# Where the next layer's modulation is computed, and how one layer's dense products are dealt among its recurrence and attention

## The chip, the cores and the metric

The kernel runs on one core of a Trainium2 chip. The metric is device time in microseconds (us) of one execution; the times below are of whole runs, the rows of one profiled execution.

## The reference

Two trunk layers over 256 latent tokens and 256 context tokens of width 1024. A layer normalises its input with an adaptive scale and shift, projects it once (`w_in`), runs three token mixers on the result (a bidirectional RWKV recurrence, a neighbourhood attention, a differential attention), merges them through sigmoid gates, projects (`w_out`), normalises and adds to its input:

```
mod_x = silu(c) @ w_mod[l] + b_mod[l]
sh_x, sc_x, gt_x = split(mod_x, 3)
hx = rmsnorm(x, g_pre[l]) * (1 + sc_x) + sh_x
z = hx @ w_in[l]
o = three branches of z, each times silu of its own gate
y = (sum_n sigmoid(mg_n) * (o_n @ w_branch[l, n])) @ w_out[l]
x = x + gt_x * rmsnorm(y, g_post[l])
...
```

The same is done for the context tokens with `c_ctx`; the last layer leaves their output out. The scale and shift of a layer depend on `c`, `c_ctx` and weights alone, not on the layer before.

## The kernel before

All matmuls run in a float32 form that splits each weight tile in two: ScalarE (ACT) writes the high part `wh`, VectorE (DVE) the remainder `wl`, and each product takes three matmuls (`mm3`: two on `wh`, one on `wl`). Weights come as 128x512 tiles (256 KB) on SyncE's (SP's) DMA queue into six buffers `wr`. A scheduler decides the order of each engine's instructions from the order in which the program writes them; each engine then runs its queue in that order and waits where an input isn't there.

A layer is written as follows (`run`). `weave` runs a main generator, `rwkv` and then `attn`, beside a fill generator: the projections of the later branches and gates (`zs`), the next layer's gate row (`mods`) and the first two merges. Main yields a weight at each of its phases, which is a debt; the fill then emits products until their own weights (a 256-column matmul group has a fixed one) pay it. The weights stand in the table `yl`, line 142 for layer 0 and line 143 for layer 1. In it `qq` is the phase after the recurrence's inverses, `step` the chunk steps of the recurrence (two numbers: first and second half of the sequence), `diff` a unit of the differential attention (its first number goes for layer 1's two row tiles; the second is not reached there), `nd` the norm of a pair of heads (first pair, second pair). What is not dealt when main ends is emitted then.

The last merge (`merge` with b=2, the branch of the differential attention) is emitted alone: four chunks of 24 matmuls of 512 columns; each channel tile's product is gated on DVE (`th`, line 192), added on POOL into `acc`, and split into high and low parts by ACT and DVE (`merged`). `outproj` then makes the output product in four chunks of 256 columns, in each of which four `in_wo` tiles are loaded, split and multiplied; after each split it calls `ahead(i)`, i = 0 to 15. Here the next layer's modulation comes in (layer 0 only): `mod_load` loads `in_wm` tiles (128x512, 32 in all) into slots of the slab on SP's queue, and `mod_rows` is a generator of four groups of 8 steps and a tail: a step is one weight tile against the 32 columns `cs` into the PSUM tile `y`, the tail adds the bias row on DVE (line 185, `k<-y,k`), transposes it on PE (line 199, `z<-cst,k`) and writes the scales and shifts (DVE line 192, `mA`, and ACT). 36 `next` exhaust it. `derived`, some small DVE instructions and one exponential for the next layer's constants, is emitted between the last merge and the product. `late`, `residual` and `norm_row` then make the next layer's input and `stream_in` transposes it for layer 1's first projections.

```
def ahead(i):
    if i % 4 == 3 and i // 4 < (2 if last else 4):
        self.rows_load(xsrc, i // 4, xs)
    if not last:
        self.mod_load(l + 1, ws, 2 * i - 4)
        for _ in range(2 if i > 6 else 0):
            next(mod)
```

Of the kernel before, what the change touches and what calls it, by code (L numbers as in the profile page):

```python
# [134 lines left out]
class K:  # L135
    def __init__(self, tc, io, out):
        self.tc, self.nc, self.io, self.out = tc, tc.nc, io, out
        self.n = 0
        self.have = {}
        self.in_order = False  # L140

        self.yl = [dict(inv=(57, 42.0), qq=(6, 12.07), step=(6, 6), na=(2.5, 1.19), diff=(2.3, 2.9), q=(1.0, 1.0), nd=(2.75, 5), A=(0, 0), B=(0, 4), G=(0.75, 0), C=(5.6, 7.2)),
                   dict(inv=(23, 51), qq=(3.0, 1.5), step=(6, 6), na=(1.0, 2.3), diff=(4.69, 8.12), q=(1.0, 1.0), nd=(0, 2), A=(0, 0), B=(4.5, 0), G=(0.75, 0), C=(4.0, 6.0))]


    def count(self):
# [1235 lines left out]
    def run(self):  # L1382
        tc, nc, io = self.tc, self.nc, self.io
        with ExitStack() as es:
# [26 lines left out]
            xs = []  # L1411
# [9 lines left out]
            ws = []  # L1421
            self.start(0, P, xs, self.mod_rows(0, P, ws), ws)
            for l in range(L):
                last = l == L - 1
                nq = NX if last else T
                acc = [None] * 8
                PN = None if last else self.params(l + 1)
# [23 lines left out]
                fill = self.chain(self.both(mods(), zs()), self.merge(l, 0, acc, nq), self.merge(l, 1, acc, nq))  # L1451
                self.weave(self.rwkv(l, P, last), fill, False)
                self.weave(self.attn(l, P, last), fill)
                self.now(self.merge(l, 2, acc, nq))
                s = self.merged(acc, nq)
                xsrc = io["xt"] if l == 0 else self.xd

                ws, xs, late = [], [], []
                if not last:
                    self.derived(l + 1, PN)  # L1460
                    self.h_new()
                    mod = self.mod_rows(l + 1, PN, ws)

                def ahead(i):
                    if i % 4 == 3 and i // 4 < (2 if last else 4):
                        self.rows_load(xsrc, i // 4, xs)
                    if not last:
                        self.mod_load(l + 1, ws, 2 * i - 4)
                        for _ in range(2 if i > 6 else 0):
                            next(mod)  # L1470

                def rows(t, y, ss):
# [4 lines left out]
                def done(t, y, ss):  # L1477
                    if t < 2:
                        rows(t, y, ss)
                    else:  # L1480
                        late.append((t, y, ss))

                self.outproj(l, s, 1 if last else 2, ahead, done)
                if not last:
                    self.mod_load(l + 1, ws, 32)
# [68 lines left out]
```

## Time and profile before

| | |
|---|---|
| median of 3 runs | 1429.24 us (1428.95 to 1432.83) |
| profiled execution | 1424.81 us |
| its span | 1423.1 us |
| TensorE (PE) busy | 1320.4 us, 93% |
| VectorE (DVE) busy | 995.7 us, 70% |
| ScalarE (ACT) busy | 779.2 us, 55% |
| GpSimd (POOL) busy | 233.6 us, 16% |
| mean granted clock of PE | 0.966 of full speed |

Busy time is the union of an engine's instructions. The span is what the trace covers; the execution's own time holds a little more around it. On the time axis of the trace the last merge of layer 0 runs from about 737 to 759 us, the output product to about 823, layer 1's first projections begin at about 833; layer 1's recurrence steps run from about 1187, its attention ends at about 1346, and its last merge and output product follow.

### The profile page before, as it was taken

The page shows a single profiled execution, that of the slowest core. Times are in us where ns is not written, and L with a number is a line of the kernel's source. Part 1 is how long each engine was busy: PE and PEld are TensorE (multiplying, and loading weights), DVE is VectorE, ACT ScalarE, POOL GpSimd, SP SyncE. Part 2 cuts the span into 40 slices and gives each one's busy share as a digit, 9 for nine tenths or more (in the row PEclk, how much of TensorE's full clock was granted, in tenths as well). Part 3 has the DMA queues.
Part 4 walks back from the last instruction along what each step waited for, and adds up shares of the span by engine and source line. Part 5 has one row for each costly group of instructions (what it writes and reads, how often), then busy time and mean ns, then how long its engine had stood idle before and what let it go on. Part 6 is the DMA issues. An engine that isn't in the chain of part 4 may idle for free. (4 is left out here: it accounts for less than half of the span.)

```text
span 1423.1 us, 28637 instructions
## 1 busy us (share of the span) xinstructions
PE 1320.4 (93%) x10784; PEld 1098.9 (77%) x10784; DVE 995.7 (70%) x2117; ACT 779.2 (55%) x1734; POOL 233.6 (16%) x292
## 2 busy tenths in 40 slices
PE   6998999999999999998999889998999999999897
PEld 4866777889779876677778777888878789867687
DVE  4763469836898368778685386768848893679886
ACT  5462375336863446667433255866449634467653
POOL 0010011012110012224253000101111000122441
PEclk9999999999999999999999999999889999999899
DMA  9466642424324267432545844354513252685454
GB/s 356 129 196 200 208 130 82 128 68 157 119 80 121 77 185 222 155 105 93 178 145 168 324 127 119 113 177 126 170 56 105 68 148 69 182 272 154 141 166 154
DMA packets 112987, 212.42 MB, mean 149 GB/s; under 512 B 13088, under 2 KB 24880, under 8 KB 112848
## 3 DMA queue, kind: packets, MB, share of 16 engines
q1 hardware_dynamic: 102896, 178.33, 40.6%
q0 software_dynamic: 9952, 32.26, 7.0%
q8 instruction: 85, 1.39, 0.4%
q14 instruction: 54, 0.44, 0.1%
HBM read 176.70 MB, written 33.83 MB: 148 GB/s over the span
## 5 line engine op out<-in xcount | busy, mean ns | idle before, releaser
L195 PE MATMUL z<-k,wh 128*128 128x512 f32 (+1 forms) x2352 | 653.9, 361 | 8.8 <-ACT wh L164 4.2
L195 PEld LDWEIGHTS z<-k,wh 128*128 128x128 f32 x2352 | 417.8, 194 | 76.2 <-issue 9.1
L195 PE MATMUL z<-k,wl 128*128 128x512 f32 (+1 forms) x1176 | 421.7, 360 | 7.3 <-DVE wl L185 7.3
L164 ACT ACTIVATE wh<-wr 128x512 fp32r<-128x512 f32 x376 | 235.4, 630 | 317.8 <-PE z L195 212.7
L185 DVE TENSOR_TENSOR wl<-wr,wh 128x512 fp32r<-128x512 f32 x376 | 278.5, 747 | 157.7 <-PE z L195 59.9
L195 PEld LDWEIGHTS z<-k,wl 128*128 128x128 f32 x1176 | 227.1, 194 | 42.8 <-DVE wl L185 12.1
L195 PE MATMUL z<-wh,k 128*128 128x256 f32 x736 | 145.1, 291 | 2.6 <-ACT k L164 1.3
L195 PEld LDWEIGHTS z<-wh,k 128*128 128x128 f32 x736 | 119.6, 196 | 5.7 <-DVE k L192 2.1
L195 PE MATMUL z<-wl,k 128*128 128x256 f32 x368 | 106.7, 290 | 0.6 <-DVE wl L185 0.6
L185 POOL TENSOR_TENSOR k<-k,k 64x512 fp32r<-64x512 f32 (+3 forms) x64 | 78.0, 1222 | 154.9 <-ACT k L164 62.1
L164 ACT ACTIVATE gs<-z 128x512 f32<-128x512 f32 (+1 forms) x134 | 66.7, 500 | 53.5 <-PE z L195 44.1
L164 ACT ACTIVATE k<-k 64x256 fp32r<-64x256 f32 (+5 forms) x146 | 74.8, 537 | 32.0 <-POOL k L185 20.3
L185 DVE TENSOR_TENSOR k<-k,k 128x256 fp32r<-128x256 f32 (+5 forms) x134 | 76.0, 580 | 12.0 <-ACT k L164 9.3
L199 PE MATMUL b<-cst,k 128*128 128x128 f32 x368 | 65.1, 286 | 17.6 <-DVE k L189 5.6
L164 ACT ACTIVATE k<-a,s 128x512 f32<-128x512 f32 (+1 forms) x96 | 59.2, 617 | 33.1 <-DVE s L179 32.1
L195 PEld LDWEIGHTS z<-wl,k 128*128 128x128 f32 x368 | 72.2, 196 | 1.4 <-DVE wl L185 1.0
L199 PEld LDWEIGHTS b<-cst,k 128*128 128x128 f32 x368 | 42.9, 144 | 37.6 <-issue 15.0
L164 ACT ACTIVATE k<-b 128x256 f32<-128x256 f32 (+1 forms) x144 | 62.8, 465 | 16.5 <-PE b L199 15.8
L195 PE MATMUL a<-k,k 128*128 128x512 f32 (+1 forms) x192 | 61.1, 404 | 10.0 <-ACT k L164 6.1
L195 PE MATMUL a<-ar,bk 64*128 64x128 f32 (+1 forms) x512 | 51.1, 288 | 9.6 <-ACT Lab L164 8.8
L195 PEld LDWEIGHTS a<-ar,bk 64*128 64x128 f32 x512 | 43.5, 190 | 21.3 <-ACT Lab L164 15.7
L179 DVE TENSOR_REDUCE s<-a 128x1 f32<-128x512 f32 (+1 forms) x96 | 56.4, 588 | 1.2 <-PE a L195 1.0
(175 smaller groups left out, 1899.4 us busy)
## 6 DMA issues: line engine op xcount, KB each, us to landing
wr<-in_wi SPq DMA_DIRECT2D x296, 256.0 KB, 3.1
k<-in_wm SPq DMA_DIRECT2D x64, 256.0 KB, 5.4
wr<-in_wb SPq DMA_DIRECT2D x48, 256.0 KB, 2.6
md<-gs SPq DMA_DIRECT2D x36, 256.0 KB, 2.9
k<-md POOLq DMA_DIRECT2D x36, 256.0 KB, 4.5
wr<-in_wg SPq DMA_DIRECT2D x32, 256.0 KB, 3.4
wr<-in_wo SPq DMA_DIRECT2D x32, 256.0 KB, 4.0
gd<-gs SPq DMA_DIRECT2D x18, 256.0 KB, 3.2
```

The lines of the kernel that those rows point to most:

```text
L164: return self.nc.scalar.activation(out=out, in_=in_, func=func, **kw)
L179: return self.nc.vector.tensor_reduce(out=out, in_=in_, axis=AX.X, op=op, **kw)
L185: return (eng or self.nc.vector).tensor_tensor(out=out, in0=a, in1=b, op=op)
L195: return self.nc.tensor.matmul(out, lhsT=lhsT, rhs=rhs, start=start, stop=stop)
L199: return self.nc.tensor.transpose(out, in_, self.ident[0:k, 0:k])
```

## The change

Two parts. In layer 0, `derived` and `mod_rows` begin ahead of the last merge. Four `in_wm` tiles are loaded before it; after each of its four chunks loads up to the 8th, 12th, 16th and 20th tile are issued and four steps of the modulation are emitted (16 in all: the first group with its tail, and seven steps of the second). In the product one load goes with each split (18 + i) instead of two (2i − 4), and one step comes at i = 2 to 11 (10 steps) instead of two at i = 7 to 15 (18). After the product 10 steps are left instead of 18. In layer 1 four numbers of the weight table that are reached change: `qq` first half 3.0 to 0, `step` second half 6 to 4.5, `diff` 4.69 to 5.86, `nd` second pair 2 to 5.0. The number of instructions on each engine stays.

```diff
@@ -140,7 +140,7 @@
         self.in_order = False
 
         self.yl = [dict(inv=(57, 42.0), qq=(6, 12.07), step=(6, 6), na=(2.5, 1.19), diff=(2.3, 2.9), q=(1.0, 1.0), nd=(2.75, 5), A=(0, 0), B=(0, 4), G=(0.75, 0), C=(5.6, 7.2)),
-                   dict(inv=(23, 51), qq=(3.0, 1.5), step=(6, 6), na=(1.0, 2.3), diff=(4.69, 8.12), q=(1.0, 1.0), nd=(0, 2), A=(0, 0), B=(4.5, 0), G=(0.75, 0), C=(4.0, 6.0))]
+                   dict(inv=(23, 51), qq=(0, 1.5), step=(6, 4.5), na=(1.0, 2.3), diff=(5.86, 16.24), q=(1.0, 1.0), nd=(0, 5.0), A=(0, 0), B=(4.5, 0), G=(0.75, 0), C=(4.0, 6.0))]
 
 
     def count(self):
@@ -1451,22 +1451,30 @@
                 fill = self.chain(self.both(mods(), zs()), self.merge(l, 0, acc, nq), self.merge(l, 1, acc, nq))
                 self.weave(self.rwkv(l, P, last), fill, False)
                 self.weave(self.attn(l, P, last), fill)
-                self.now(self.merge(l, 2, acc, nq))
+                ws, xs, late = [], [], []
+                if last:
+                    self.now(self.merge(l, 2, acc, nq))
+                else:
+
+                    self.derived(l + 1, PN)
+                    mod = self.mod_rows(l + 1, PN, ws)
+                    self.mod_load(l + 1, ws, 4)
+                    for i, _ in enumerate(self.merge(l, 2, acc, nq)):
+                        self.mod_load(l + 1, ws, 4 * i + 8)
+                        for _ in range(4):
+                            next(mod)
                 s = self.merged(acc, nq)
                 xsrc = io["xt"] if l == 0 else self.xd
 
-                ws, xs, late = [], [], []
                 if not last:
-                    self.derived(l + 1, PN)
                     self.h_new()
-                    mod = self.mod_rows(l + 1, PN, ws)
 
                 def ahead(i):
                     if i % 4 == 3 and i // 4 < (2 if last else 4):
                         self.rows_load(xsrc, i // 4, xs)
                     if not last:
-                        self.mod_load(l + 1, ws, 2 * i - 4)
-                        for _ in range(2 if i > 6 else 0):
+                        self.mod_load(l + 1, ws, 18 + i)
+                        if 2 <= i < 12:
                             next(mod)
 
                 def rows(t, y, ss):
```

SP's queue in the product of layer 0: `wr<-in_wo` are its weights, `k<-in_wm` the modulation's, `k<-in_xt` rows of the input. Before, from the end of the second bunch of `in_wm`:

```order
L167 DMA k_9008<-in_wm 128x512
L167 DMA k_9010<-in_wm 128x512
L167 DMA wr_9044<-in_wo 128x512
L167 DMA k_9050<-in_xt 128x512
L167 DMA k_9051<-in_xt 128x512
L167 DMA k_9054<-in_wm 128x512
L167 DMA k_9056<-in_wm 128x512
L167 DMA wr_9109<-in_wo 128x512
L167 DMA k_9115<-in_wm 128x512
L167 DMA k_9117<-in_wm 128x512
L167 DMA wr_9133<-in_wo 128x512
L167 DMA k_9139<-in_wm 128x512
```

and in the change, from the last three chunks' loads on:

```order
L167 DMA k_9076<-in_wm 128x512
L167 DMA wr_9106<-in_wo 128x512
L167 DMA k_9112<-in_wm 128x512
L167 DMA wr_9142<-in_wo 128x512
L167 DMA k_9148<-in_xt 128x512
L167 DMA k_9149<-in_xt 128x512
L167 DMA k_9152<-in_wm 128x512
L167 DMA wr_9198<-in_wo 128x512
L167 DMA k_9204<-in_wm 128x512
L167 DMA wr_9212<-in_wo 128x512
L167 DMA k_9218<-in_wm 128x512
L167 DMA wr_9226<-in_wo 128x512
```

`wr_9044`, the twelfth `in_wo` of the product, stood behind sixteen `in_wm`; the eleventh and twelfth of the change, `wr_9106` and `wr_9142`, have one `in_wm` ahead of each. Further up the change's queue, in the last merge, the second `in_wo` of the second chunk stands behind eight `in_wm` in a row.

DVE's queue around the modulation's first row add (`k<-y,k` 128x128); `wl<-wr,wh` are splits of weights, `y<-a,k` and `y<-z,k` products with the gate row in `outproj`, 128x512 of line 192 the gated products of the merge. Before, in the third chunk of the product:

```order
L185 TENSOR_TENSOR wl_9047<-wr_9044,wh_9046 128x512
L185 TENSOR_TENSOR y_8604<-a_8749,k_8591 128x256
L185 TENSOR_TENSOR y_8605<-a_8750,k_8595 128x256
L185 TENSOR_TENSOR y_8606<-a_8750,k_8595 128x256
L185 TENSOR_TENSOR wl_9112<-wr_9109,wh_9111 128x512
L185 TENSOR_TENSOR wl_9136<-wr_9133,wh_9135 128x512
L185 TENSOR_TENSOR k_8867<-y_8869,k_8867 128x128
L185 TENSOR_TENSOR wl_9160<-wr_9157,wh_9159 128x512
L192 SCALAR_TENSOR_TENSOR mA_8870<-z_9059,pc_946 128x2 x2
```

and in the change, in the last merge:

```order
L192 SCALAR_TENSOR_TENSOR k_8380<-k_8380,a_8402 128x512
L192 SCALAR_TENSOR_TENSOR k_8383<-k_8383,b_8462 128x512
L185 TENSOR_TENSOR wl_8592<-wr_8589,wh_8591 128x512
L192 SCALAR_TENSOR_TENSOR k_8384<-k_8384,z_8477 128x512
L185 TENSOR_TENSOR wl_8598<-wr_8595,wh_8597 128x512
L185 TENSOR_TENSOR k_8425<-y_8427,k_8425 128x128
L192 SCALAR_TENSOR_TENSOR k_8458<-k_8458,a_8532 128x512
L185 TENSOR_TENSOR wl_8724<-wr_8721,wh_8723 128x512
L192 SCALAR_TENSOR_TENSOR k_8459<-k_8459,b_8547 128x512
L192 SCALAR_TENSOR_TENSOR mA_8428<-z_8571,pc_946 128x2
```

The first row add now stands among the merge's gated products, behind the split of the last merge weights instead of splits of the third chunk's output weights.

PE's queue at the last scores of layer 1's attention: `a<-k,k` 128x512 are scores, `y<-k,k` values, `b<-cst,k` transposes. Before:

```order
L195 MATMUL a_15751<-k_15443,k_15442 128x512 x2
L195 MATMUL a_15761<-k_15451,k_15450 128x512 x2
L199 MATMUL b_15774<-cst,k_15640 128x128 x4
L195 MATMUL a_15827<-k_15671,k_15670 128x512 x2
L195 MATMUL a_15837<-k_15679,k_15678 128x512 x2
L195 MATMUL y_15857<-k_14874,k_15779 128x128
L195 MATMUL y_15857<-k_14875,k_15779 128x128
L195 MATMUL y_15857<-k_14878,k_15779 128x128
L195 MATMUL y_15857<-k_14879,k_15779 128x128
L199 MATMUL b_15850<-cst,k_15756 128x128 x4
L195 MATMUL a_15999<-k_15671,k_15670 128x512 x2
L195 MATMUL a_16009<-k_15679,k_15678 128x512 x2
```

and in the change:

```order
L195 MATMUL z_15750<-k_8693,wl_15802 128x256
L195 MATMUL z_15750<-k_8694,wh_15801 128x256
L195 MATMUL z_15750<-k_8702,wh_15801 128x256
L195 MATMUL z_15750<-k_8694,wl_15802 128x256
L195 MATMUL a_15827<-k_15635,k_15634 128x512 x2
L195 MATMUL a_15837<-k_15643,k_15642 128x512 x2
L199 MATMUL b_15850<-cst,k_15724 128x128 x4
L195 MATMUL y_15857<-k_14778,k_15747 128x128
L195 MATMUL y_15857<-k_14779,k_15747 128x128
L195 MATMUL y_15857<-k_14782,k_15747 128x128
L195 MATMUL y_15857<-k_14783,k_15747 128x128
L195 MATMUL a_15999<-k_15635,k_15634 128x512 x2
```

The scores `a_15827` were preceded by transposes of the pair before; now they are preceded by the last of a block of 43 fill matmuls, `z<-k,wh` and `z<-k,wl`.

Counted in these orders, the fill matmuls of layer 1 that stand ahead of the same instruction of main:

| main instruction | before | change |
|---|---|---|
| first inverse product after the inverses, second half | 1308 | 1284 |
| first recurrence step, values | 1338 | 1314 |
| second step, first product | 1386 | 1332 |
| third step, first product | 1434 | 1386 |
| first scores of attention | 1572 | 1512 |
| scores in the middle | 1684 | 1624 |
| scores `a_15645` (before's name) | 1847 | 1781 |
| scores `a_15751` and `a_15761` | 1848 | 1800 |
| scores `a_15827` and all behind | 1848 | 1848 |

## Rows read from the trace of the kernel before

**Rows 1.** Busy us (and instructions) of PE, PEld, DVE, ACT, POOL; PEclk, DMA share, GB/s.

```profile
738.00:759.00 21.00, 21.00 (x94) 17.13 (x93) 12.83 (x19) 5.73 (x10) 12.77 (x14) 1.00 0.56 178
759.00:772.00 13.00, 10.90 (x84) 10.12 (x83) 7.20 (x16) 4.24 (x8) 7.01 (x7) 1.00 0.34 91
772.00:797.00 25.00, 24.95 (x247) 23.34 (x245) 8.29 (x24) 6.90 (x23) 1.19 (x2) 1.00 1.01 346
797.00:803.00 6.00, 0.86 (x11) 0.39 (x9) 2.01 (x4) 1.60 (x3) 0.00 (x0) 0.82 0.99 340
803.00:808.00 5.00, 5.00 (x31) 4.68 (x24) 1.35 (x4) 2.10 (x8) 0.00 (x0) 0.53 1.04 378
...
823.00:833.00 10.00, 7.28 (x139) 5.57 (x132) 8.32 (x38) 5.12 (x17) 1.08 (x2) 0.76 0.45 155
...
1172.00:1200.00 28.00, 27.00 (x517) 26.05 (x518) 11.77 (x14) 11.29 (x19) 1.54 (x1) 0.94 0.26 77
...
1183.30:1186.50 3.20, 3.20 (x19) 3.20 (x16) 0.00 (x0) 1.18 (x2) 0.00 (x0) 0.50 0.02 5
...
1320.00:1329.00 9.00, 8.71 (x63) 7.57 (x62) 8.04 (x15) 8.71 (x22) 3.85 (x4) 1.00 0.35 97
1329.00:1346.00 17.00, 10.99 (x52) 7.74 (x51) 14.18 (x41) 10.48 (x28) 10.00 (x13) 0.80 0.48 155
```

**Rows 2.** Timeline of PE in the output product: start, us, operation, [idle before <-releaser].

```profile
796.79 0.28 PE L195 MATMUL z<-wl,k 128*128 128x256 f32 x1
796.91 0.28 PE L195 MATMUL z<-wh,k 128*128 128x256 f32 x1
802.33 0.48 PE L199 MATMUL z<-cst,k 128*128 128x128 f32 x1 [5.14 <-DVE k L185]
```

**Rows 3.** Timeline of DVE, same place.

```profile
795.11 0.69 DVE L185 TENSOR_TENSOR wl<-wr,wh 128x512 fp32r<-128x512 f32 x1 [9.23 <-ACT wh L164]
...
801.38 0.69 DVE L185 TENSOR_TENSOR wl<-wr,wh 128x512 fp32r<-128x512 f32 x1 [1.31 <-ACT wh L164]
801.99 0.28 DVE L185 TENSOR_TENSOR k<-y,k 128x128 f32<-128x128 f32 x1
```

**Rows 4.** Timeline of ACT, same place.

```profile
794.44 0.63 ACT L164 ACTIVATE wh<-wr 128x512 fp32r<-128x512 f32 x1 [9.02 <-DMA wr<-in_wo]
```

**Rows 5.** Timeline of SP's DMA queue, last merge to product.

```profile
738.77 33.48 SPq L167 DMA_DIRECT2D wr<-in_wo  x11
...
773.25 8.49 SPq L167 DMA_DIRECT2D k<-in_wm  x8
...
789.09 0.33 SPq L167 DMA_DIRECT2D wr<-in_wo  x1
```

**Rows 6.** Timeline of PE, first chunk of the output product.

```profile
758.99 0.28 PE L195 MATMUL z<-wh,k 128*128 128x256 f32 x1
...
770.50 0.38 PE L195 MATMUL z<-wh,k 128*128 128x256 f32 x1 [1.28 <-ACT k L164]
...
773.47 0.28 PE L195 MATMUL z<-wh,k 128*128 128x256 f32 x1
```

**Rows 7.** Timeline of POOL, one of six adds alike.

```profile
768.20 1.58 POOL L185 TENSOR_TENSOR k<-k,k 128x512 f32<-128x512 f32 x1 [2.13 <-DVE k L192]
```

**Rows 8.** Timeline of PE, modulation matmuls in and after the product.

```profile
786.22 0.64 PE L195 MATMUL y<-k,cs 128*32 128x128 f32 x16
786.79 0.39 PE L195 MATMUL z<-wh,k 128*128 128x256 f32 x1
...
822.77 1.95 PE L195 MATMUL y<-k,cs 128*32 128x128 f32 x64
```

**Rows 9.** The page, part 6: DMA issues.

```profile
k<-in_wm SPq DMA_DIRECT2D x64, 256.0 KB, 5.4
```

**Rows 10.** Timeline of DVE, a recurrence step of layer 1.

```profile
1194.51 2.14 DVE L185 TENSOR_TENSOR UV<-ht,PC 64x512 f32<-64x512 f32 x2
```

**Rows 11.** Timeline of PE, last heads of layer 1's attention.

```profile
1335.52 1.22 PE L195 MATMUL a<-k,k 128*128 128x512 f32 x2 [2.28 <-ACT k L164]
```

## The prediction

> **What bounds the kernel now.** I read the page first, then the busy time by stretch around the two places that the change touches, then the engine timelines inside each. TensorE (PE) is busy 93% of the span, so the time goes where PE waits, where its clock is low, or where work can be taken from it; the edits touch only the border of layers 0 and 1 and layer 1's order, and the number of matmuls is the same. What counts is PE's waiting in those places.
>
> At the border, the stretches [rows 1] show three different things. In the last merge (738 to 759) PE is full while the DMA engines are at 0.56; in 759 to 772 they are at 0.34 and PE is busy 10.90 of 13 us; in 772 to 797 PE is full and the DMA share is 1.01. Then, at 797 to 803, PE does 0.86 us of work in 6, and from 803 to 808 its granted clock is 0.53, the lower of its two levels. PE's timeline names the hole: after the product matmul at 796.91 it waits 5.14 us for a DVE result, the transpose of the first modulation row group [rows 2]. DVE's timeline says why: that row add (801.99, 0.28 us) stands in its queue behind splits of output weights, which wait for ScalarE (9.23 us for the first) [rows 3], and ScalarE waits 9.02 us for the DMA of in_wo [rows 4]. SyncE's queue closes the chain: eleven in_wo loads are issued by 772.2, then in_wm loads in two bunches of eight, the first of which holds the queue for 8.49 us, and the twelfth in_wo goes out at 789.09 only [rows 5]. So the row add does not wait for its own sums; it waits for weights that were issued late, behind modulation weights.
>
> A smaller hole lies ahead of it: the first chunk of the product begins at 758.99 and its last matmul starts at 773.47; PE's waits in it (the longest 1.28 us) are for splits on DVE and ScalarE [rows 6]. They come from a cycle: each gated sum on POOL waits 2.13 us for a DVE split [rows 7], some 3.7 us with the add's own 1.58, where PE needs 12 matmuls for the same tile, 2.7 us by the pace of the merge (94 in 21 us [rows 1]).
>
> **The change, part by part.** Lost time at the border first. (a) The stall: 5.14 us of waiting, and 5 us at a clock of 0.53 behind it, of which 0.47 is lost, 2.35 us [rows 1, 2]; 7.5 in all. The order of the change has no in_wm bunch ahead of the in_wo of the last two chunks: they alternate one to one, and the first row group's add comes in the merge, where weights are early. I take −7.5, and as bounds −7.5 and 0 (the wait appears again elsewhere).
> (b) The first chunk: 14.6 us against 96 × 0.12 = 11.5 (the pace from the starts 796.79 and 796.91 [rows 2]), so 3.0 lost. In the new order the multiplies that feed POOL's adds stand ahead of the splits that closed the cycle. I take −3.0, bounds −3.0 and 0.
> (c) Added ahead of the product's end: 24 modulation steps with matmuls instead of 16, in 13 insertions instead of 9. Eight steps alone take 1.95 us, 0.24 each; two between products take 0.57 us from their start to the next product (786.22 to 786.79), a little more with the change over to them [rows 8]: I take 0.25 a step and 0.2 an insertion. 8 × 0.25 + 4 × 0.2 = +2.8, all of it on PE where it is full. The 8 steps saved after the product gain nothing there: in 823 to 833 PE is busy 7.28 of 10 us and waits for the norm chain [rows 1].
> (d) derived: thirteen small DVE instructions (2.3 us) move ahead of the merge's weight splits. DVE is busy 12.83 of 21 us there [rows 1], so between 0 and 2.3; I take +0.7.
> (e) The moved loads: SyncE issues twenty in_wm between the last in_wb and the first in_wo loads, and the modulation's row load goes out on POOL's queue behind its first two adds (up to 1 us of POOL, hidden: the rows are wanted at the first tail). An in_wm lands 5.4 us after its issue [rows 9]. By this the second group of sums may be wanted up to 2 us before its weights are there; +0.5, bounds 0 and 2.
> (f) The tail after the product keeps ten steps. Between one row add fewer and a quieter PE I take 0.
> Together −7.5 − 3.0 + 2.8 + 0.7 + 0.5 = **−6.5** for the border.
>
> Layer 1 next. In the new order some 60 dense matmuls of the layer's fill stand later than before from the first recurrence steps through attention until the second last head, and 61 come in front of the last scores, where there were none. (g) 60 × 0.12 = 7.2 us go from a stretch where PE is busy 27.00 of 28 us [rows 1]. What covers is lost at one place: the first step's fill falls from 48 matmuls to 18, 2.2 us, beside a DVE pair of 2.14 us that the next products wait for [rows 10], so nothing is left to spare there; other such places I cannot see, and count a quarter of the 7.2 as cover lost: −5.4, bounds −7.2 and −3.0. (h) The 61 cost 7.3 us in the last heads. There PE is busy 10.99 of 17 us at a clock of 0.80, DVE 14.18 [rows 1], and the largest wait is 2.28 us for ScalarE [rows 11]. The largest block, 43 of them, stands ahead of that pair of scores, so I let 3.6 of the 6.0 idle us be filled, that wait and what lies next to it; the low clock costs at most 0.20 × 11 = 2.2 us, of which half comes back: 7.3 − 3.6 − 1.1 = +2.6. Bounds: all idle time filled and the clock full, −0.9; nothing hidden, +7.3. Layer 1: **−2.8**.
>
> The sum is −9.3 us. The profiled execution took 1424.81 us (its span 1423.1), which becomes 1415.5; the median of the runs stands 4.4 us above it, so the forecast is **1419.9 us**. About 0.3%, 4.3 us, is what a measurement of this kernel can tell from no change: below 1424.9 is faster, above 1433.5 slower.
>
> **The rivals.** *The loads crowd the merge.* It moves 178 GB/s × 21 us = 3.7 MB now, and twenty in_wm are 5.2 MB more: 8.9 MB in the 27 us to 765 are 330 GB/s, near the 346 GB/s of the stretch with a full DMA share [rows 1]. If they land as late as the in_wo did there, the four groups of sums in the merge wait some 1.1 us each, 4.3 us, and the border gives −2.2: 1424.2. For it: the arithmetic leaves 5%. Against: the loads are spread over four chunks. Chance 0.12. The Trainium skill (DMA: Bandwidth & Descriptors, "Issuing engines are not separate DMA queues") says that transfers share the same 16 engines whoever starts them; by this POOL's moved row load would queue with the rest as well.
> *Layer 1's moved work is not hidden.* DVE's 14.18 of 17 us may be what sets the end there; then (h) is +7.3, layer 1 +1.9, the sum −4.6: 1424.6; with (g) at its weak end +4.3 and 1427.0. Chance 0.13.
> *Layer 1 gains more*: (h) mostly under idle time, −6: 1416.7. Chance 0.07.
> *A quiet tail.* With half the steps left after the product PE waits longer for the norm chain. What the rows show: 5.14 us of waiting were followed by a clock of 0.53 [rows 1, 2], and the stretch 823 to 833 has 0.76. If the low clock now reaches the first 4 us of layer 1's products, 2 us come back: 1421.9. Chance 0.08. The Trainium skill (TensorE: Matmul & The Clock Gate, "HAM oscillation") says that waits between bursts of matmuls bring the array back to its slow clock; by this rule the border would gain 4.5 instead of 6.5. The clock of 0.76 in that stretch agrees with the rule in kind.
> *The change does not do what it says.* The second in_wo of the second chunk stands behind eight in_wm in a row; if those hold the queue as the eight in [rows 5] did (8.49 us), the stall moves forward to the second chunk, and (b) is used up by (c): about 0 at the border, and 1426.4 in all. Chance 0.06.
> *Slower.* Modulation matmuls have 32 columns of weights; the clock may fall at each insertion. Behind layer 1's small 32x32 matmuls it is 0.50 for 3.2 us [rows 1], which costs 1.6 us. 13 insertions at 1.5 us are +19.5, the sum +10.2: 1439.4. It loses from 7 of the 13 on and is measurably slower from 10. Against it: 772 to 797 holds four insertions at a clock of 1.00 [rows 1]. Chance 0.04.
>
> **How the numbers follow.** The forecast has what is left, 0.50, with its own range of 1415 to 1424. The range of 8 in 10 takes in, above, the crowded merge and the unhidden layer 1 at once (−2.2 + 1.9, 1428.9), and below, a border without (d) and (e) and without a price of the insertions (−7.5 − 3.0 + 2.0) beside a layer 1 at its two lower bounds (−8.1): −16.6, 1412.6. Faster: the forecast, the better layer 1, the quiet tail and about half of the two rivals between 1424.2 and 1427.0, 0.77. Same: the rest of these and the change that doesn't work, 0.18. Slower: the clock, and a little for cases not thought of, 0.05.
>
> **What would show it.** In the changed kernel's profile: no wait over 1 us for the modulation's transpose in the product, no in_wo issued more than 8 us after the one before it, a clock of 1.00 from the merge to the product's end (else the slow rival); DMA share near 1 in the merge and lower in the product; PE waiting on modulation sums in the merge would show the crowding. In layer 1, PE's idle time in the last 17 us of attention falls from 6.0 to about 2.4 us and the clock there rises over 0.9; if the last heads get longer by 7 us instead, (h) was wrong. I am wrong if the border takes as long as before, or if layer 1's last heads grow by more than its first steps shrink.

## The result, and the profile after

The changed kernel takes 1411.53 us (median of 4 runs, 1405.38 to 1413.47) against 1429.1 us of the kernel before in the same comparison: a ratio of 0.9868, interval 0.9829 to 0.9906, or 18.9 us less (13.4 to 24.4). The forecast was 1419.9 us with a range from 1412.6. The direction was right; the gain that was forecast, 9.3 us, is half of the measured one, and the median lies 1.1 us below the range.

The profiled execution took 1413.47 us (span 1411.8), 11.3 us less than the profiled one of before. That pair is not a good measure of the whole: the code up to the last merge of layer 0 is the same, and there the second one is 8.5 us behind (its last merge begins at 745.5, before's at 737.0), with more stretches at the low clock. So I compare stretches that begin and end at the same instruction. All stretches below do. Low clock stands for the time at the lower level, worked out as 2 × (1 − PEclk) × length; where PE is busy all through it, it costs half of it, and less where PE would have waited anyway.

Of the border, busy time by part of the kernel after: last merge, the four chunks of the output product, the tail up to layer 1's first product, the first 120 of its products, and the rest to a mark in layer 1 (900 us in before). Columns: length, busy time (and instructions) of PE, PEld, DVE, ACT, POOL, PEclk, DMA share, GB/s.

```profile
745.50:773.80 28.30, 27.18 (x218) 20.53 (x216) 21.60 (x41) 9.74 (x20) 16.96 (x17) 1.00 0.84 305
773.80:786.50 12.70, 12.70 (x117) 12.04 (x113) 7.66 (x14) 4.82 (x13) 4.45 (x5) 1.00 0.71 228
786.50:800.20 13.70, 13.70 (x133) 12.36 (x129) 4.30 (x9) 4.34 (x13) 0.00 (x0) 1.00 1.06 387
800.20:813.40 13.20, 13.20 (x124) 12.21 (x121) 4.12 (x9) 3.83 (x11) 0.00 (x0) 1.00 0.41 125
813.40:824.80 11.40, 11.40 (x97) 11.40 (x96) 8.23 (x32) 5.44 (x18) 1.14 (x2) 1.00 0.21 70
824.80:834.60 9.80, 4.64 (x79) 3.44 (x78) 8.79 (x39) 5.95 (x19) 1.08 (x2) 0.77 0.52 161
834.60:856.20 21.60, 18.09 (x133) 16.91 (x131) 17.90 (x55) 12.68 (x29) 0.00 (x0) 0.95 0.38 110
856.20:901.80 45.60, 43.60 (x194) 35.96 (x195) 29.62 (x62) 24.53 (x48) 5.48 (x9) 0.93 0.43 119
```

The same view of the kernel before, its first and third chunk and the last stretch:

```profile
759.00:773.60 14.60, 12.50 (x98) 11.72 (x97) 8.46 (x24) 4.93 (x11) 8.20 (x8) 1.00 0.39 104
...
786.80:808.90 22.10, 16.96 (x158) 15.15 (x154) 5.32 (x13) 5.97 (x19) 0.00 (x0) 0.85 1.03 371
...
854.30:900.00 45.70, 43.66 (x193) 36.07 (x194) 29.68 (x63) 24.57 (x48) 5.44 (x8) 0.93 0.42 123
```

The hole of [rows 2] and the low clock behind it ([rows 1], 803 to 808) are gone: PE is full at full clock from the first to the last chunk, and the third chunk takes 13.2 us instead of 22.1. The waits of the first chunk [rows 6] are gone too. The merge carries the modulation and takes 28.3 us instead of 22. Whole border: 156.3 us against 163.0 (737.0 to 900.0), 6.7 less.

PE's waits from the merge to layer 1's first products, after (what waited for what: us in total, times, longest):

```profile
PE a L199 <- ACT k L164: 3.4, 1, 3.4
PE z L199 <- DVE k L185: 1.7, 1, 1.7
PE z L195 <- DVE k L185: 1.1, 2, 0.8
```

The first two lie in the tail, where PE waits for the norm chain (3.4 us; before, the same wait was 0.5 us). The third is new, in the merge.

Layer 1, from its inverses to the end of its first two merges, by stretch. Before:

```profile
1021.80:1048.70 26.90, 26.86 (x479) 21.23 (x480) 7.98 (x11) 13.62 (x24) 3.03 (x3) 0.75 0.33 97
1048.70:1076.40 27.70, 25.86 (x308) 22.58 (x308) 17.85 (x34) 15.74 (x37) 4.27 (x5) 0.94 0.14 39
1076.40:1173.00 96.60, 89.39 (x618) 79.28 (x618) 84.84 (x183) 60.70 (x134) 9.18 (x13) 0.96 0.38 114
1173.00:1193.80 20.80, 20.80 (x451) 19.89 (x453) 6.60 (x9) 7.75 (x13) 0.00 (x0) 0.92 0.20 60
1193.80:1243.50 49.70, 46.96 (x716) 43.98 (x712) 31.26 (x56) 25.13 (x48) 5.52 (x5) 1.00 0.52 150
1243.50:1323.40 79.90, 74.55 (x481) 59.05 (x482) 69.51 (x143) 56.77 (x147) 23.54 (x28) 0.96 0.67 204
1323.40:1341.10 17.70, 13.15 (x68) 10.09 (x67) 14.33 (x34) 13.25 (x33) 8.48 (x11) 0.81 0.39 120
1341.10:1390.00 48.90, 43.64 (x335) 41.53 (x334) 41.43 (x98) 24.39 (x56) 18.45 (x22) 0.97 0.56 171
```

After:

```profile
1023.40:1051.30 27.90, 27.90 (x490) 22.27 (x491) 9.46 (x21) 13.72 (x25) 2.54 (x2) 0.76 0.28 85
1051.30:1074.00 22.70, 22.46 (x291) 19.55 (x290) 16.58 (x25) 16.26 (x37) 3.90 (x5) 1.00 0.21 60
1074.00:1167.00 93.00, 86.54 (x613) 77.40 (x614) 83.42 (x181) 59.71 (x134) 8.93 (x13) 0.98 0.38 114
1167.00:1186.40 19.40, 19.40 (x441) 18.41 (x443) 6.42 (x9) 7.13 (x12) 0.00 (x0) 0.82 0.22 70
1186.40:1232.50 46.10, 42.83 (x680) 39.63 (x676) 28.73 (x52) 21.96 (x41) 5.57 (x5) 1.00 0.47 133
1232.50:1308.50 76.00, 71.38 (x477) 58.09 (x478) 68.16 (x143) 56.52 (x146) 24.01 (x28) 0.98 0.67 211
1308.50:1330.10 21.60, 19.16 (x133) 16.67 (x132) 18.45 (x39) 16.52 (x41) 9.05 (x11) 1.00 0.51 154
1330.10:1379.00 48.90, 44.42 (x336) 41.74 (x335) 41.26 (x99) 25.54 (x56) 18.27 (x22) 0.97 0.57 182
```

The stretches are: inverses of the first half, its recurrence steps, the second half's groups, its inverses, its steps, attention, the last heads, and the rest. Their sum fell from 368.2 to 355.6 us, by 12.6. As many fill matmuls come back in the last heads as leave ahead of them, so the work is the same, and the 12.6 should be waits and clock: PE's idle time is 27.0 us before (368.2 less the busy 341.2) and 21.5 after, 5.5 less; the low clock is 43.8 us before and 30.0 after, 13.8 less, worth at most 6.9. Both together are at most 12.4. Counted on PE's busy time alone the low clock is 41.0 and 30.6 us, worth 5.2; some 2 us are then left that neither explains.

### The profile page after: what moved, and what is told of

Read it like the earlier page. It is cut to its first block, busy times and chain, and to the rows that moved or that the text cites. A ratio compares the mean times of both kernels' runs of the same rounds, so it can differ in the third digit from the quotient of the medians.

```text
span 1411.8 us, 28621 instructions
## 1 busy us (share of the span) xinstructions
PE 1316.8 (93%) x10784; PEld 1096.9 (78%) x10784; DVE 997.7 (71%) x2117; ACT 780.3 (55%) x1734; POOL 234.1 (17%) x292
## 4 chain that ended last, share of the span: by engine, by line
PE 61%; DVE 18%; ACT 11%; DMA 6%; issue 4%; SPq 0%; DVEq 0%; POOL 0%; ACTq 0%; POOLq 0%
PE z L195 39%; PE a L195 12%; ACT k L164 6%; PE y L195 5%; DVE wl L185 4%; DVE k L185 3%; PE b L195 3%; PE b L199 2%; DMA wr<-in_wi 2%; DVE X L182 2%; DVE k L192 2%; ACT wh L164 1%; DVE s L179 1%; DMA k<-in_wm 1%; DMA k<-in_nb 1%
## 5 line engine op out<-in xcount | busy, mean ns | idle before, releaser
L195 PEld LDWEIGHTS z<-k,wl 128*128 128x128 f32 x1176 | 228.1, 195 | 45.9 <-DVE wl L185 14.4
L164 ACT ACTIVATE k<-b 128x256 f32<-128x256 f32 (+1 forms) x144 | 62.7, 466 | 15.2 <-PE b L199 14.6
L195 PE MATMUL a<-k,k 128*128 128x512 f32 (+1 forms) x192 | 58.1, 390 | 5.7 <-DVE k L185 2.4
L195 PEld LDWEIGHTS a<-ar,bk 64*128 64x128 f32 x512 | 42.1, 187 | 22.2 <-ACT Lab L164 16.6
```

Source lines behind the costliest of these rows:

```text
L164: return self.nc.scalar.activation(out=out, in_=in_, func=func, **kw)
L195: return self.nc.tensor.matmul(out, lhsT=lhsT, rhs=rhs, start=start, stop=stop)
```

## The experiments

Each ran beside the kernel before on the same chip: e1 to e4 on one, e5 to e8 on a second, e9 to e12 on a third, e13 and e14 on a fourth. Ratios are to that kernel; us are the ratio's, with its interval.

**The two parts apart.** One kernel has the layer-0 part alone, one has layer 1's weights alone, two have a pair of these weights. Of the table's line only the numbers that change are shown.

```diff
-qq=(3.0, 1.5), step=(6, 6)
+qq=(0, 1.5), step=(6, 4.5)          # e2, e3
-diff=(4.69, 8.12), nd=(0, 2)
+diff=(5.86, 16.24), nd=(0, 5.0)     # e2, e4
```

> The layer-0 part alone, layer 1's weights as before. Theory A (the parts add, layer 1 was mis-sized): the border gives the forecast 6.5 us and no more, 6 to 8 us under the kernel before, near 1422. Rival B (layer 1's gain in the profiled pair is half chance of the clock, the border is worth more than forecast): 11 to 13 us under it, near 1417. In the profile, for both: no wait over 1 us for the modulation's transpose inside the product, the product's first chunk without waits, and a longer wait for the norm chain behind the product, about 3.5 us.

> Layer 1's weights alone, layer 0 as before. Theory A: 10 to 13 us under the kernel before, near 1418: the 60 moved products cost their 7.2 us in full where they stood, two of three waits for the recurrence's Lab tiles go, and the last heads take them in for about 3 us. Rival B: 4 to 6 us under it, near 1424, the rest of the profiled pair's difference being half-clock stretches that lay elsewhere by chance. The stall of 5 us in layer 0's product stays.

> Of layer 1's weights only qq (3.0 to 0) and step (6 to 4.5). The recurrence has 54 to 60 fill matmuls fewer, and the attention's weights are not raised, so some 29 of them are left behind the last scores. Theory A: the gain up to the attention is all there, 8 us, and the last heads lose less than 3 us: 6 to 9 us under the kernel before, near 1421. Rival B: 3 us under it, near 1426.

> Of layer 1's weights only diff (4.69 to 5.86) and nd (2 to 5.0): the recurrence's fill is as before, and 72 to 96 matmuls of the first two merges come in front of the last scores instead of behind them (8.6 to 11.5 us of work). Theory A: they fill at most the 6 us in which PE was idle there: 3 to 5 us under the kernel before, near 1425. Rival B (the end of the attention is set by VectorE, 14.2 of 17 us busy): no change within 2 us, near 1429.

| run | ratio (interval) | us |
|---|---|---|
| e1_border | 0.9985 (0.9966 to 1.0004) | −2.1 (−4.8 to +0.6) |
| e2_layer1 | 0.9905 (0.9886 to 0.9924) | −13.5 (−16.3 to −10.8) |
| e3_qq_step | 0.9931 (0.9913 to 0.9948) | −9.8 (−12.4 to −7.4) |
| e4_diff_nd | 1.0045 (1.0025 to 1.0065) | +6.4 (+3.6 to +9.3) |

Layer 1's weights alone bring most of the gain, and its stretches have the lengths of the whole change within 0.2 us in both traces: theory A's size holds there (13.5 us where it said 10 to 13), and rival B falls. The same goes for e3 (9.8 us; theory A 6 to 9). The border alone brings less than either theory said. In its trace the border is as long as in the whole change; what differs is the measure. The border in e1, and with the old border in e5:

```profile
736.00:892.10 156.10, 144.34 (x1074) 124.77 (x1073) 102.10 (x255) 71.15 (x163) 28.99 (x34) 0.96 0.55 184
743.60:902.60 159.00, 143.58 (x1074) 125.71 (x1073) 97.66 (x253) 69.44 (x161) 29.61 (x35) 0.97 0.56 188
```

In six traces with the old border (e2 to e7) it is 159.0 to 159.5 us, not 163.0: the last stretch, layer 1's first projections, is 42.6 us long there instead of before's 45.7, with no low clock in it, and the stall of the third chunk is 3.3 to 4.3 us long instead of 5.1. So the profiled execution of before had some 4 us in its border that the kernel does not usually have, and by the traces the usual gain of the border is 3 us. The timing's interval holds that, and holds no gain at all as well.

The raised weights of the last heads (e4) are a miss for both theories. The last heads, 17.7 us before, and the rest, 48.9, in e4:

```profile
1327.40:1359.90 32.50, 25.16 (x165) 22.28 (x164) 22.48 (x51) 18.88 (x46) 9.46 (x13) 0.84 0.50 154
1359.90:1399.00 39.10, 32.56 (x240) 30.67 (x239) 32.77 (x82) 18.46 (x41) 16.32 (x20) 0.91 0.43 135
```

The merges' matmuls that came forward lengthen the heads by 14.8 us and shorten the rest by 9.8: they fill no idle time (7.3 us of it stay in the heads), and the clock stays low. Without qq and step there is nothing left to deal at that point but the merges; with them, the same weights deal the projections left over, and are worth the difference of e2 to e3, some 3.7 us, in the timing.

**The first half's steps.** e5 sets qq to 0 alone, e6 step to 4.5 alone, e7 qq to 6.0 alone; e12 is the whole change with qq at 6.0.

```diff
-qq=(3.0, 1.5), step=(6, 6)
+qq=(0, 1.5), step=(6, 6)            # e5
+qq=(3.0, 1.5), step=(6, 4.5)        # e6
+qq=(6.0, 1.5), step=(6, 6)          # e7
+qq=(6.0, 1.5), step=(6, 4.5)        # e12, with all else of the change
```

> Of layer 1's weights only qq (3.0 to 0): 8 to 12 fill matmuls fewer in the first half's recurrence steps, 1.0 to 1.4 us of work, all of it back by the attention. Theory P (the fill's weight splits stand in VectorE's queue ahead of the recurrence's own chain; fewer of them free the chain, take PE's waits away and keep its clock up): the stretch from the first step of the first half to the first group of the second shrinks from 27.7 us to about 23, as with all of layer 1's new weights; the kernel gains 4 to 8 us, near 1420. Rival Q (the matmuls' own time is the gain): that stretch shrinks by 1.4 us, and the kernel stays within 2 us, near 1425.

> Of layer 1's weights only step of the second half (6 to 4.5): up to 24 fill matmuls fewer in the second half's steps, dealt out again by the middle of the attention. Theory P: the first half's stretch keeps its 27.7 us; from the second half's steps to the attention 3 to 4 us go, of which the attention gives back about 2: 1 to 4 us under the kernel before, near 1424. Rival Q: 24 times 0.12, 2.9 us less ahead of the attention and as much more in it, no change within 2 us.

> The reverse of the last but one: qq 3.0 to 6.0, some 4 to 7 fill matmuls more in the first half's steps and up to 30 more ahead of the second half's. Theory P: the first half's stretch does not shrink and the waits in it stay or grow, 27 to 31 us; the second half's steps and the attention have the same low clock as before; the kernel is 2 to 6 us slower than before, near 1430. Rival Q: work only changes its place, within 2 us of the kernel before.

> The whole change with qq of the first half at 6.0 instead of 0: as many fill matmuls as before the change or more up to the attention, but the second half's steps at 4.5 and the raised weights of the last heads. Theory P (fewer fill matmuls in the first half's steps take the waits away): the stretch of the first half's steps is back at 26 to 28 us with 2 us of waits, and the kernel loses 4 to 6 us of the whole change, near 1413. Rival R (what counts is how the fill meets the phases, not its amount; qq at 6.0 alone gained 8 us): it gains as much as the whole change or up to 3 us more, 1405 to 1409.

| run | ratio (interval) | us | steps of the first half |
|---|---|---|---|
| e5_qq | 0.9968 (0.9951 to 0.9986) | −4.6 (−7.0 to −2.0) | 22.8 |
| e6_step | 0.9973 (0.9952 to 0.9995) | −3.8 (−6.8 to −0.7) | 27.7 |
| e7_qq_more | 0.9941 (0.9918 to 0.9965) | −8.4 (−11.7 to −5.0) | 26.8 |
| e12_qq6_all | 0.9923 (0.9898 to 0.9947) | −11.0 (−14.5 to −7.6) | 26.7 |

The stretch of e5, against 27.70 us before:

```profile
1052.40:1075.20 22.80, 22.57 (x293) 19.64 (x293) 16.66 (x25) 16.28 (x37) 3.89 (x5) 1.00 0.20 59
```

It is 4.9 us shorter: 1.6 us of PE's waits go, 3.4 us of low clock, worth 1.7, and 1.7 us of work. That work is not fill. Both stretches have 81 fill matmuls; what has left are 15 small matmuls of the attention's rows (transposes and products of two columns), which now stand among the inverses ahead of it and make these 0.9 us longer. The fill that was not dealt is missing on either side, in the inverses and in the second half's groups. So the expected fall to 23 us came, but not by fewer fill matmuls in the stretch.

VectorE's and PE's timelines at the stretch's first step show one of the three waits that go. Before, the split of a fill weight (`wl`) stands between the two instructions of the recurrence (`ht`, `UV`), and PE then waits for `UV`:

```profile
1048.67 0.69 DVE L185 TENSOR_TENSOR ht<-a,H 128x512 f32<-128x512 f32 x1 [5.71 <-PE a L195]
1049.28 0.68 DVE L185 TENSOR_TENSOR wl<-wr,wh 128x512 fp32r<-128x512 f32 x1
1049.87 2.25 DVE L185 TENSOR_TENSOR UV<-ht,PC 64x512 f32<-64x512 f32 x2
...
1051.55 0.30 PE L195 MATMUL a<-UV,k 128*64 128x64 f32 x2 [0.67 <-DVE UV L185]
```

After, the split stands behind `UV`, and an instruction of the attention's rows has taken its place. PE does not wait:

```profile
1051.26 0.69 DVE L185 TENSOR_TENSOR ht<-a,H 128x512 f32<-128x512 f32 x1 [3.29 <-PE a L195]
1051.87 0.68 DVE L185 TENSOR_TENSOR k<-k,b 128x512 f32<-128x512 f32 x1
1052.47 1.88 DVE L185 TENSOR_TENSOR UV<-ht,PC 64x512 f32<-64x512 f32 x2
1054.37 0.69 DVE L185 TENSOR_TENSOR wl<-wr,wh 128x512 fp32r<-128x512 f32 x1
```

This does not show theory P's mechanism. The instruction that took the split's place is as long (0.68 us), and `UV` starts 1.20 us after `ht` both times. What differs is that the pair of `UV` takes 1.88 us instead of 2.25, and that PE has matmuls for 2.4 us after `ht` instead of 2.2. Why the other two waits go (both on ScalarE, 0.5 us each) was not settled.

P's length for this stretch comes true in e5, e6 and e12; e7 is a little below it (26.8, forecast 27 to 31). But P also said that the waits hold the clock down, and e7 and e12 speak against that. There 1.6 us of waits stay and the clock is full; e7:

```profile
1052.20:1079.00 26.80, 25.17 (x315) 22.13 (x314) 17.34 (x34) 15.83 (x36) 4.04 (x5) 1.00 0.17 50
```

e12 gains 4.5 us less than the same change timed beside it (e11 below), as P said and rival R did not, though the two intervals overlap. P fails for e7 as a whole: the waits stay, as it said, but the kernel gains 8 us where a loss was expected. So a lower `qq` is one way to a faster layer, not a rule; what made e7 faster was not settled (its profiled execution was the slowest of its seven).

**The border in pieces.** e8 puts `derived` back behind the merge, e9 emits the product's modulation steps in pairs, e10 takes the kernel before with the loads' new pace alone, e11 is the whole change once more.

```diff
-                    self.derived(l + 1, PN)                                  # e8, ahead of the merge
+                    self.derived(l + 1, PN)                                  # e8, behind it
...
-                        if 2 <= i < 12:
-                            next(mod)
+                        for _ in range(2 if i in (2, 4, 6, 8, 10) else 0):   # e9
+                            next(mod)
...
+                    self.mod_load(l + 1, ws, 4)                              # e10
+                    for i, _ in enumerate(self.merge(l, 2, acc, nq)):
+                        self.mod_load(l + 1, ws, 4 * i + 8)
...
-                        self.mod_load(l + 1, ws, 2 * i - 4)
+                        self.mod_load(l + 1, ws, 18 + i)
```

> The whole change, but the next layer's derived constants stay behind the last merge, where they were. The forecast took 0.7 us for moving them ahead of the merge; in the profile PE waits 1.1 us for VectorE at the merge's start. So that wait goes, the merge takes 27.2 us instead of 28.3, and the kernel gains about 1 us on the whole change, which the clock can hide. Rival: the constants, now among the splits for the product's first chunk, bring back the waits in that chunk (up to 3 us), and nothing is gained. This run also shows a third time whether the new border has a low clock in layer 1's first projections.

> The whole change, with the ten modulation steps of the output product in five pairs (i = 2, 4, 6, 8, 10) instead of ten single ones: five insertions fewer. In the traces a single step costs 0.54 us in the product and a pair 0.71, so an insertion costs 0.25 to 0.3 over its work, where the forecast took 0.2. So the product shrinks by 5 times 0.28, some 1.4 us less the tail step's share, and the kernel gains about 1 us on the whole change, 19 to 20 us under the kernel before. Rival (the clock decides): the shift of 1 us moves the low-clock stretch in layer 1's first projections, and up to 3 us more come or go there.

> The kernel before with the changed pace of the modulation's loads alone (20 of the 32 in the last merge, then one with each split); the modulation's steps, derived and layer 1's weights stay as before. Theory (the stall in the product's third chunk is late output weights, not the place of the steps): the wait of 5 us is gone, the third chunk takes 14 to 15 us instead of 21 to 22, and the border shrinks by 7 us of that alone; in the timing 3 to 7 us, since the clock in layer 1's first projections can take 3 back. Rival (the row add must come earlier): the wait stays over 3 us, no change within 2 us. The first chunk keeps its 2.1 us of waits under either, as the multiplies' place stays.

> The whole change again, on the same chip as the three others, as their measure. If the parts add: border 2 to 3.5 and layer 1 13.5 under the kernel before, 16 to 18 us in all, near 1409. Segments of the profile as in the first one: border 156.3 us up to the 900 us mark, layer 1 from its inverses to the end of the merges 355 to 356.

| run | ratio (interval) | us |
|---|---|---|
| e8_derived | 0.9870 (0.9842 to 0.9897) | −18.5 (−22.5 to −14.7) |
| e9_pairs | 0.9869 (0.9844 to 0.9894) | −18.7 (−22.2 to −15.1) |
| e10_loads | 0.9940 (0.9922 to 0.9959) | −8.6 (−11.1 to −5.8) |
| e11_after_again | 0.9891 (0.9868 to 0.9915) | −15.5 (−18.8 to −12.1) |

e8: the merge keeps its 28.3 us and its 1.2 us of waits, so `derived` is not their cause, and its place costs nothing that shows; its ratio is from another chip than that of e11. e9: the product takes 49.7 us instead of 51.0, the 1.3 us that were expected; in the timing it cannot be told, as the whole change itself stands at 0.9868 and 0.9891. e10: the loads' pace alone takes the stall away, and the third chunk is 14.4 us (22.1 before):

```profile
783.60:798.00 14.40, 14.40 (x157) 13.08 (x153) 4.74 (x12) 4.62 (x16) 0.00 (x0) 1.00 0.63 210
```

It gains more than the whole border part (their intervals do not meet). The first chunk's waits go as well, which was not expected, as the program's text leaves the multiplies where they were. But the scheduler makes another order of it. Before, DVE's queue in the merge alternates between the gated products (`k<-k,b` and the like) and the high and low splits of their sums (`k<-k,k`), which wait for ACT:

```profile
748.09 0.69 DVE L192 SCALAR_TENSOR_TENSOR k<-k,k 128x512 fp32r<-128x512 f32 x1 [1.95 <-ACT k L164]
748.70 0.68 DVE L192 SCALAR_TENSOR_TENSOR k<-k,b 128x512 f32<-128x512 f32 x1
...
751.83 0.69 DVE L192 SCALAR_TENSOR_TENSOR k<-k,k 128x512 fp32r<-128x512 f32 x1 [1.85 <-ACT k L164]
```

In e10, as in the change, four more of the products stand ahead of the first split:

```profile
752.24 0.69 DVE L192 SCALAR_TENSOR_TENSOR k<-k,a 128x512 f32<-128x512 f32 x1 [1.75 <-DMA k<-md]
...
753.96 0.69 DVE L192 SCALAR_TENSOR_TENSOR k<-k,b 128x512 f32<-128x512 f32 x1 [0.43 <-PE b L195]
...
755.17 1.78 DVE L192 SCALAR_TENSOR_TENSOR k<-k,k 128x512 fp32r<-128x512 f32 x1
```

**Without the moved steps.** e13 is e10 with layer 1's new weights; e14 also moves each bunch of loads one chunk later, so that the first four come behind the merge's first chunk, and sixteen instead of twenty in the merge.

```diff
-                    self.mod_load(l + 1, ws, 4)
                     for i, _ in enumerate(self.merge(l, 2, acc, nq)):
-                        self.mod_load(l + 1, ws, 4 * i + 8)
+                        self.mod_load(l + 1, ws, 4 * i + 4)                  # e14
```

> The whole change without its moved steps: the loads paced as in the change and layer 1's new weights, the modulation's steps and derived where they were before. If the moved steps cost more than they bring (pacing alone gained 8.5 us, the whole border part 2.1): 8.5 and 13.5 add up to 22 us under the kernel before, near 1404, and the border is 153 us up to the 900 us mark. Rival (the border part's small timing was the clock's chance, and moved steps cost nothing): as the whole change, 16 to 19 us under the kernel before, near 1408.

> As the run beside it, with the first four modulation loads behind the merge's first chunk instead of ahead of the merge's last weights. Theory (PE's 1.2 us of waiting in the last merge come from those four loads, which stand ahead of the last merge weights on SyncE's queue): the merge is back at 22 us without waits, and the kernel gains 1.2 us on the run beside it. Rival (the wait has another cause): the merge keeps 23.5 us.

e13: 0.9839 (0.9810 to 0.9868), 23.0 us less (18.8 to 27.1), 1403.26 us. e14: 0.9833 (0.9807 to 0.9859), 23.8 us less (20.1 to 27.5), 1402.88 us. Both are ahead of the kernel before, and the two parts add: 8.6 and 13.5 are 22.1. They gain 4 to 8 us more than the change did in its two timings, but on another chip, and their intervals overlap with that of its first one. What the traces show is that e13's border is 153.4 us long, where it is 155.4 to 156.3 in the five with the moved steps as in the change (the change's own, e1, e8, e11 and e12). Merge, third chunk and tail of e13:

```profile
736.10:759.70 23.60, 22.38 (x97) 17.83 (x96) 17.85 (x23) 8.17 (x14) 16.27 (x16) 1.00 0.86 312
...
784.20:798.60 14.40, 14.40 (x157) 13.08 (x153) 4.74 (x12) 4.62 (x16) 0.00 (x0) 1.00 0.65 207
...
812.30:823.40 11.10, 7.92 (x143) 6.23 (x141) 8.84 (x41) 5.56 (x18) 1.08 (x2) 0.85 0.43 144
```

From the merge to the tail's end e13 takes 87.3 us (736.1 to 823.4), the change 89.1 (745.5 to 834.6): the steps moved ahead of the product's end cost PE 4.7 us in the merge, and the shorter product and tail give back 2.9. The merge of e14:

```profile
740.10:762.10 22.00, 22.00 (x97) 17.94 (x96) 17.79 (x21) 8.19 (x14) 15.10 (x16) 1.00 0.87 312
```

The 1.2 us of waits are gone. e14 moves all bunches, but of the change's loads only the first four are issued ahead of the two waits (at 746.2 and 750.5 us); in SyncE's queue they stand ahead of the merge's last weights, and the next `in_wm` follow at 752.7:

```profile
738.21 1.53 SPq L167 DMA_DIRECT2D wr<-in_wb  x2
739.79 1.85 SPq L167 DMA_DIRECT2D k<-in_wm  x4
742.33 0.33 SPq L167 DMA_DIRECT2D wr<-in_wb  x1
745.63 7.01 SPq L167 DMA_DIRECT2D wr<-in_wo  x3
```

## Why the prediction was wrong, point by point

**The step that failed is layer 1's sum, (g) above all.** It had −5.4 + 2.6 = −2.8; the pair of traces shows −12.6, the timing of that part alone −13.5. (g) priced 60 matmuls at their own 0.12 us and took a quarter off for lost cover, with −7.2 as the best case. But since the same matmuls return later, their own time is no gain; the gain is what the other engines and the clock give, and I bounded that from one side only. Ahead of the last heads (1021.8 to 1323.4) the layer lost 16.5 us where (g) had 5.4: 7.9 of moved work (66 matmuls by then), 2.6 of PE's waits (17.2 to 14.6) and at most 3.5 for the low clock (34.2 to 27.1 us); 2.5 us or more of it I cannot assign. I had read the stretch at 1172 to 1200 alone [rows 1], which is nearly full, and taken it for all; the steps of the first half, 1.8 us idle of 27.7 at a clock of 0.94, were not looked at. Why fewer waits and less low clock come with the new numbers is open: in e5 both go, in e7 and e12 only the low clock. (h) was nearer: the last heads grew by 3.9 us where +2.6 was forecast, with the idle time falling from 4.6 to 2.4 us and the clock rising to 1.00, as the text's last part asked for.

**The border's sum was right for the pair of traces and too large for the kernel.** −6.5 was forecast, 163.0 to 156.3 is −6.7, and that they agree is luck. Term by term: (a) came in full, no wait for the modulation's transpose is left in the product and its clock is 1.00; the cause named, late in_wo behind in_wm, is shown by e10, and where the row add stands does not matter for it. (b) came, with the order of DVE's queue that it named; but it is the loads' pace that makes this order, not the moved steps (e10). No run has the one without the other. (c) was somewhat small: single steps cost 0.54 us each in the product (13.7 us for 96 products of 0.12 and four steps), pairs 0.7 (12.9 us with two in the second chunk of e13), so an insertion costs 0.2 to 0.3 over its work of 0.24 a step. The merge grew by 5.2 us (28.3 less 22.0 and 1.1 of waits) for its fifteen steps in four insertions, and the product is 1.6 us shorter than e13's (51.0 against 52.6): +3.6, where +2.8 was forecast. (d) is 0 by e8. (e) is 1.1 us, not 0.5, and has another place: not the sums wait for their weights, but the merge, at its start, behind the first four loads (e14). (f): idle time in the tail rose from 2.7 to 5.2 us, but the part is 9.8 us long after 10.5; in the six other traces with the old border it is 9.8 us too.
What made the sum too large is its base. All of it was made against one execution, whose 163.0 us held some 20 us of low clock at this place; the six others hold 10 to 14 and take 159.0 to 159.5. Against those the change gains 3 us.

**The rivals.** The loads did not crowd the merge in the way described: no sum waits for its weights, at a DMA share of 0.84 and 305 GB/s; an in_wm lands 5.9 us after issue instead of 5.4 [rows 9]. The quiet tail came about in kind: PE waits 3.4 us for the norm chain, the clock is 0.77 in the tail and 0.93 in the last stretch of the border. It is not settled whether that stretch is slow because of the tail: it has 6.8 us of low clock in three traces of the new border (the change's own, e1, e8), 3.4 in two (e11, e12), none in one (e9), none in the six with the old one and 6.8 in the first of before. The Trainium skill (TensorE: Matmul & The Clock Gate, "HAM oscillation") says that waits between bursts of matmuls bring the slow clock back. For this speaks that the tail and the first 120 products behind it have together 6.8 us of low clock in all six traces of the new border, with the wait of 3.4 us, and 3.4 in the six of the old one; against it, that they have 6.8 in e10 and e13 as well, where no wait in the tail is longer than 1.8 us. The slow clock after each insertion did not come: 1.00 through 13 insertions. The stall's return at the second chunk did not come either. Its condition did: eight in_wm hold SyncE's queue for 8.47 us (from 760.05), and twice an in_wo goes out over 8 us after the one before it, which had been named as a sign of failing; but PE waits for none of them. The DMA share was not near 1 in the merge (0.84), and not lower in the product's second chunk (1.06), as had been expected.

**The chances.** 0.77 stood on faster, which came true. The range ended at 1412.6, 1.1 us above the median, which is less than the timing can tell. Its lower end was made of layer 1's two best cases, −8.1, and that is the bound that did not hold.

## What to carry to other kernels

When fill work is moved from one place to another, its own time cancels; what is won or lost is waits and low clock in the stretches that it leaves and enters, so look at every one of them, not at the fullest. When loads are moved, compare the order of the other engines' queues too: a scheduler can change it, as it did for DVE in e10. When loads stand in front of other loads on one queue, change their pace first and alone: here that was worth more than moving the computation too. And before a sum is made against one profiled execution, see in a second one whether its low clock lies at the same places.

## What the runs showed of the hardware

The same unchanged 737 us of the program took 8.5 us longer in one profiled execution than in another, with 41 us of low clock instead of 24 and PE's waits nearly alike (31.9 and 30.5 us without the first one of 11.3). Over all sixteen traces this part takes 733.5 to 745.5 us with 17 to 41 us of low clock: 12 us of time for 24 of low clock, which is the half that was reckoned above. Stretches without such a difference repeat within 0.2 us over all traces (the second half's steps: 46.1 or 46.2 us in all traces with the new `qq` and `step`). A small set of matmuls put between others (eight of 32 columns) cost 0.2 to 0.3 us over its own time, at an unchanged clock of 1.00.
